# One-hots of a decoder layer's expert selection: each token's values contiguous, indices and gates held twice

## The chip, the cores and the metric

The kernel runs on one core of one Trainium2 chip. Time is device time of one execution in microseconds. Before the change the median of three runs is 1737.91 us (1737.27 to 1738.87). One execution was recorded by the hardware profiler; all rows and traces below come from such recordings.

## The reference

One decoder layer for 256 tokens of width 2048: an input projection, two groups of attention heads, an output projection with residual and LayerNorm, then retrieval over 128 x 128 = 16384 experts of one neuron each, and a second LayerNorm. What matters here is the retrieval:

```python
qh = (xc @ wq).reshape(TOKEN_CHUNK, PEER_HEADS, 2, PEER_HALF)
s1 = jnp.einsum('chd,nd->chn', qh[:, :, 0], sk1)      # 128 scores, s2 likewise
v1, i1 = lax.top_k(s1, PEER_TOPK)                     # 16 best of each half
cand = v1[..., :, None] + v2[..., None, :]
cidx = i1[..., :, None] * PEER_NKEYS + i2[..., None, :]
top_s, pos = lax.top_k(cand, PEER_TOPK)               # 16 of the 256 sums
eidx = jnp.take_along_axis(cidx, pos, axis=-1)
g = jax.nn.softmax(top_s, axis=-1)
h = jnp.einsum('cd,chkd->chk', xc, u[eidx])
a = jax.nn.gelu(h) * g
y = jnp.einsum('chk,chkd->cd', a, v[eidx])
```

So each token selects 8 heads x 16 = 128 experts, each with a gate g. An expert's number is i1 * 128 + i2.

## The kernel before

All names and lines are those of the program printed at the end of this section. Operations are recorded through a helper (line 116), so profile rows carry line 116 and are told apart by the names of tiles; a trailing number is cut from a name there (`oh1` and `oh2` are `oh`, `iota16` is `iota`).

**Dense stream.** The work is a list of units, each one block of 1 MB of weights. A unit is loaded by SyncE's DMA queue (`raw`), split into a high and a low part (`wh` by a ScalarE cast, `wl` by a VectorE subtraction of 128 x 1024, two per unit) and multiplied on TensorE in four steps of 8 f32 matmuls (`psb<-xx,wh` and `psb<-xx,wl`). A load is issued three units ahead, a split is made two units ahead. At a unit's end ScalarE and VectorE fold its result (`ev`, `bl`). The first 32 units of the retrieval (`use_u`) take all tokens against 32 x 128 experts; the units after them (`use_c`) take gathered rows of the remaining experts, which only a list names; their weights are turned by four TensorE transposes per step.

**Jobs between the steps.** Small work is written as generators. After each step of a unit the recorder calls `pump` (line 235), which lets a job go one piece on, if a planner's clocks (`Paced`, lines 71 to 118) say that ScalarE and VectorE are no more than a slack behind TensorE, and if the job's own due time has passed. The clocks advance by a cost formula for each operation (`cost`, line 78). So the costs that the formula gives set the order in which instructions stand; the chip runs each engine's instructions in that order.

**Where the planner's order is overridden.** When a unit needs indices that the list has not given yet, `column` (line 179) calls `pump` without a slack until it has them. There the jobs are written one after the other with no dense work between; this text calls such a place a hold.

**The gates** (`job_gate`, line 878). For every token and every one of its 128 slots the kernel has i1, i2 and g. Transposed, slots lie on the 128 partitions: `iT` [128, 2, 256] holds i1 and i2 in f16, one value per token; `gpc` [128, 2, 256] holds the gate times 2^15 as an f16 value and an f16 remainder.

**One-hots** (`one_hots`, line 933). For a group of four tokens VectorE makes `oh2`, where i2 equals 0..127, and `oh1`, where i1 does; where gates are wanted also `og`, which is `oh1` times each of the two parts of the gate. `oh2` is [128, 4, 128]: a token's 128 values are neighbours. `oh1` is [128, 128, 4]: the four tokens are innermost, so a token's 128 values lie 4 elements apart; its comparison is against a table `iotab` that holds each number four times. `og` is [128, 2, 128, 4] in the same way.

**Products.** Per token, TensorE multiplies `oh2` (as weights) by `oh1` and adds over tokens: how often each expert is selected (`job_count`, line 978; 4 matmuls per group). By `og`, main part and remainder, it makes the token's 128 x 128 table of gates (`gate_mm`, 8 matmuls per group), which ScalarE copies to `stg`. All are of 128 columns. After 32 groups `stg` goes to memory in 16 stores of 512 KB (`gtab`, `job_store`, line 968) on SyncE's queue, which also issues the units' loads. `job_count` walks all 64 groups, with gates for the first 32 only; its products run two groups behind its one-hots, `oh1` and `oh2` have three buffers, `og` two. `job_gates` (line 1001) makes the other 32 groups of gates later, between list rounds.

**The list** (`job_list`, line 1020). From the counts VectorE sorts the experts, and then, in rounds, names 3 x 128 of them at a time: comparisons `sg`, f16 matmuls `psa<-dx,sg` of 130 neighbouring columns, a copy `i2l` on ScalarE, and four VectorE instructions (`at`, `lw`). One copy `i2l` marks one round.

Of the kernel before, what the change touches and what calls it, by code (L numbers as in the profile page):

```python
# [13 lines left out]
F16 = mybir.dt.float16  # L14
# [3 lines left out]
OP = mybir.AluOpType  # L18
AX = mybir.AxisListType

P = 128
S = 256
# [99 lines left out]
def layer_kernel(ctx: ExitStack, tc: tile.TileContext, xT, x, win, wo, wq, ut, un, v, lams, sublng,  # L122
# [4 lines left out]
    PE, ACT, DVE, POOL = (Paced(e, n, clk, done_at) for e, n in ((nc.tensor, "PE"), (nc.scalar, "ACT"),  # L127
                                                       (nc.vector, "DVE"), (nc.gpsimd, "POOL")))
# [11 lines left out]
    def psA():  # L140
        return pa.tile([P, 512], F32, name="psa", tag="a")

    def psB():
        return pb.tile([P, 512], F32, name="psb", tag="b")
# [733 lines left out]
    def job_gate():  # L878
        while keep.get("nhead", 0) < NH:
            yield  # L880
        s = tv2.rearrange("p t h k -> p (t h) k")
        w = tk.tile([P, 2 * NH, 16], F32, name="w")
        DVE.tensor_tensor(w, s, s[:, :, 0:1].to_broadcast([P, 2 * NH, 16]), op=OP.subtract)
        ACT.activation(w, w, AF.Exp)
        DVE.tensor_copy(ei, eid.rearrange("p t h k -> p t (h k)"))
        eh = tk.tile([P, 2, 2, P], I32, name="eh")
        DVE.tensor_scalar(eh[:, 0], ei, 7, None, op0=OP.logical_shift_right)
        DVE.tensor_scalar(eh[:, 1], ei, P - 1, None, op0=OP.bitwise_and)
        DVE.tensor_copy(i12, eh)
        yield  # L890
        DVE.tensor_reduce(gs, w, axis=AX.X, op=OP.add)
        DVE.reciprocal(gs, gs)
        DVE.tensor_tensor(w, w, gs[:, :, None].to_broadcast([P, 2 * NH, 16]), op=OP.mult)
        yield
        for t in range(2):
            ps = psA()
            for i in range(2):
                PE.transpose(ps[:, i * P:(i + 1) * P], i12[:, i, t], ident)
            PE.transpose(ps[:, 2 * P:3 * P], w.rearrange("p (t h) k -> p t (h k)", t=2)[:, t], ident)
            c = slice(t * P, (t + 1) * P)  # L900
            ACT.copy(iT[:, :, c], ps[:, :2 * P].rearrange("p (i s) -> p i s", i=2))
            ACT.copy(gT[:, c], ps[:, 2 * P:3 * P])
            yield
        DVE.tensor_scalar(gT, gT, GSCALE, None, op0=OP.mult)
        DVE.tensor_copy(gpc[:, 0], gT)
        DVE.tensor_tensor(gpc[:, 1], gT, gpc[:, 0], op=OP.subtract)
        keep["gate"] = True
        yield

# [22 lines left out]

    def one_hots(q, gated):

        k = slice(4 * q, 4 * q + 4)
        oh2 = main.tile([P, 4, P], F16, name="oh2", tag="oh2", bufs=3)
        oh1 = main.tile([P, P, 4], F16, name="oh1", tag="oh1", bufs=3)
        DVE.tensor_tensor(oh2, iota16[:, None].to_broadcast([P, 4, P]), iT[:, 1, k, None].to_broadcast([P, 4, P]),
                          op=OP.is_equal)
        DVE.tensor_tensor(oh1, iotab, iT[:, 0, None, k].to_broadcast([P, P, 4]), op=OP.is_equal)  # L940
        og = None
        if gated:
            og = main.tile([P, 2, P, 4], F16, name="og", tag="og", bufs=2)
            DVE.tensor_tensor(og, oh1[:, None].to_broadcast([P, 2, P, 4]),
                              gpc[:, :, None, k].to_broadcast([P, 2, P, 4]), op=OP.mult)
        return oh2, oh1, og

    def gate_mm(oh2, og):
        ps = psA()
        for c in range(4):  # L950
            for p in range(2):
                PE.matmul(ps[:, c * P:(c + 1) * P], oh2[:, c], og[:, p, :, c], start=(p == 0), stop=(p == 1))
        return ps

    def gate_out(gp, q, ps):

        t, k = divmod(4 * q, P)
        if k == 0:
            stgs[t] = gp.tile([P, NEXP, P], F32, name="stg", tag="stg", bufs=1)
        stg = stgs[t]  # L960
        ACT.activation(stg[:, :, k:k + 4].rearrange("p j c -> p c j"), ps.rearrange("p (c j) -> p c j", c=4), AF.Copy,
                       scale=1.0 / GSCALE)
        if k == P - 4:
            start(job_store(t, stg))
# [13 lines left out]
    def job_count(gp):  # L978


        cnt, ohs, ps, n = psA(), {}, {}, S // 4
        for q in range(n + 2):
            if q < n:
                ohs[q] = one_hots(q, q < n // 2)
            r = q - 2
            if r >= 0:
                oh2, oh1, og = ohs.pop(r)
                for c in range(4):
                    t, k = divmod(4 * r + c, P)
                    PE.matmul(cnt[:, t * P:(t + 1) * P], oh2[:, c], oh1[:, :, c], start=(k == 0), stop=(k == P - 1))  # L990
                if og is not None:
                    ps[r] = gate_mm(oh2, og)
            if r - 1 in ps:
                gate_out(gp, r - 1, ps.pop(r - 1))
            yield -1.0e9
        c2 = cnt[:, :2 * P].rearrange("p (t j) -> p t j", t=2)
        DVE.tensor_scalar(some, c2, 0.5, None, op0=OP.is_gt)
        DVE.tensor_scalar(once, c2, 1.0, None, op0=OP.is_equal)
        keep["count"] = True
# [477 lines left out]
    for n, (part, b) in enumerate(order):  # L1477
        one = part[0] == "S"
        add_unit(None, use_v(n, one, halves[n]), kind="S" if one else "V", part=part, b=b, halves=halves[n],
                 s=int(part[1]) * NS + b if one else 0)  # L1480
# [18 lines left out]

    main = ctx.enter_context(tc.tile_pool(name="main", bufs=1))  # L1500
    iota16 = main.tile([P, P], F16, name="iota16")
    iotab = main.tile([P, P, 4], F16, name="iotab")
    iT = main.tile([P, 2, S], F16, name="iT")
    gpc = main.tile([P, 2, S], F16, name="gpc")
    some = main.tile([P, 2, P], F16, name="some")
    once = main.tile([P, 2, P], F16, name="once")
    row = main.tile([P, P], F32, name="row")
# [21 lines left out]
    gT = tk.tile([P, S], F32, name="gT")  # L1529

    POOL.iota(iota50, pattern=[[1, NCAND]], base=0, channel_multiplier=0, allow_small_or_imprecise_dtypes=True)
    POOL.iota(iota16, pattern=[[1, P]], base=0, channel_multiplier=0, allow_small_or_imprecise_dtypes=True)
    POOL.iota(iotab, pattern=[[1, P], [0, 4]], base=0, channel_multiplier=0, allow_small_or_imprecise_dtypes=True)
    SP.dma_start(gtab[PADROW:, 0:P], zero.bitcast(F32))
    SP.dma_start(gtab[PADROW:, P:S], zero.bitcast(F32))
    run_units(n_wq, SLACK_TOPK)
# [5 lines left out]
    with tc.tile_pool(name="gp", bufs=1, side="right") as gp:  # L1542
        st["gates"] = pos["k"] + 2
        start(job_list(ls))
        start(job_count(gp))
        start(job_gates(gp))
        while "gates" not in keep:
            run_units(pos["k"] + 1, SLACK_GATE)
# [24 lines left out]
    with tc.If(again > 0):  # L1573
        xf = [strm.tile([P, D], F32R, name=f"w{i}", tag=f"w{i}") for i in "hl"]
        for t in range(2):
            xr = strm.tile([P, D], F32, name="raw", tag="raw")
            SP.dma_start(xr, x1d[t * P:(t + 1) * P])
            for q in range(4):
                ps = psA()
                for i in range(4):  # L1580
                    k = 4 * q + i
                    PE.transpose(ps[:, i * P:(i + 1) * P], xr[:, k * P:(k + 1) * P], ident)
                ACT.copy(xf[t].bitcast(F32)[:, q * 512:(q + 1) * 512], ps)
        for j in range(NEXP):
# [4 lines left out]
            ps = psB()  # L1589
            for t in range(2):  # L1590
                for k in range(NK):
                    c = slice(k * P, (k + 1) * P)
                    PE.matmul(ps[:, t * P:(t + 1) * P], wr[:, c], xf[t].bitcast(F32)[:, c],
                              start=(k == 0), stop=(k == NK - 1))
# [6 lines left out]
        for j in range(NEXP):  # L1601
# [4 lines left out]
            for t in range(2):  # L1606
                for c in range(4):
                    PE.matmul(yps[t][c], ar[:, t * P:(t + 1) * P], vr[:, c * 512:(c + 1) * 512],
                              start=(j == 0), stop=(j == NEXP - 1))
# [61 lines left out]
```

## Time and profile before

| what | value |
|---|---|
| median of 3 runs | 1737.91 us |
| profiled execution | 1734.11 us |
| its span, first to last instruction | 1732.2 us |
| TensorE clock granted, mean | 0.968 |
| busy: TensorE, VectorE, ScalarE, GpSimd | 93%, 75%, 47%, 34% of the span |
| counting, with gates | about 588 to 680 us |
| counting, without gates | about 680 to 739 us |
| sort of the list | about 739 to 777 us |
| gates of the other 32 groups | 817 to 938 us |

A row of the chain or the timeline gives start, length, engine, line, operation, tiles written and read, shapes and count; in brackets stands how long the engine was idle before it and what ended that. A row of a stage gives its ends, its length, and the busy time and count of each engine, then granted clock, DMA share and GB/s. A row of a tile gives the count and the shortest, median and longest duration in ns. Durations of neighbouring instructions overlap, so what an instruction costs its engine is read from start to start.

### The profile page before, as it was taken

How to read it: one execution, taken by the hardware profiler on the slowest of the kernel's cores; microseconds unless marked ns; L12 is line 12 of the kernel's file. 1: busy time of each engine (PE TensorE's matmuls, PEld its weight loads, DVE VectorE, ACT ScalarE, POOL GpSimd, SP SyncE). 2: the span in 40 equal slices, each digit the busy share in tenths (PEclk: the TensorE clock that was granted, in tenths of full speed). 3: DMA queues.
4: the chain of work that ended last, by engine and by line, in shares of the span. 5: the costliest groups of instructions: out<-in, count | busy, mean ns of one | idle time of the engine just before them, and what ended most of it. 6: DMA issues, size and time to landing. Idle time of an engine off the chain costs nothing.

```text
span 1732.2 us, 25235 instructions
## 1 busy us (share of the span) xinstructions
PE 1606.4 (93%) x9151; PEld 1364.4 (79%) x9151; DVE 1307.0 (75%) x2844; ACT 817.7 (47%) x1370; POOL 596.5 (34%) x558
## 2 busy tenths in 40 slices
PE   7999999998989899959979899999979999999994
PEld 6888888877878788849969788888857777788872
DVE  5686767656999887875976667786678888777767
ACT  5445555445424565323635333344445555555533
POOL 0033100015778400002001033334566666556742
PEclk9999999999989999979979899999999999999998
DMA  7454454545444434926324878798999999998861
GB/s 275 163 178 146 150 190 147 217 178 194 161 147 165 171 110 132 300 68 208 111 74 154 250 287 341 272 392 311 419 351 406 387 389 381 372 331 310 300 255 55
DMA packets 112531, 409.18 MB, mean 236 GB/s; under 512 B 11216, under 2 KB 62608, under 8 KB 69648
## 3 DMA queue, kind: packets, MB, share of 16 engines
q0 software_dynamic: 37856, 246.96, 37.4%
q1 hardware_dynamic: 74400, 160.27, 27.2%
q8 instruction: 74, 1.21, 0.3%
q14 instruction: 57, 0.47, 0.1%
q10 hardware_dynamic: 144, 0.26, 0.0%
HBM read 376.00 MB, written 31.39 MB: 235 GB/s over the span
## 4 chain that ended last, share of the span: by engine, by line
PE 64%; DVE 20%; DMA 6%; issue 4%; ACT 3%; POOL 2%; SPq 0%; DVEq 0%; ACTq 0%; POOLq 0%
PE psa L116 34%; PE psb L116 31%; DVE wl L116 6%; DVE oh L116 2%; ACT wh L116 2%; POOL gsr L187 1%; DMA gr<-gtab,aidx 1%; DMA sr<-x1d,xidx 1%; DVE lw L116 1%; DMA raw<-in_v_dram,vidx 1%; DVE tv L116 1%; DVE ti L116 1%; DVE yacc L116 1%; DVE eid L116 1%; DVE og L116 1%
## 5 line engine op out<-in xcount | busy, mean ns | idle before, releaser
L116 PE MATMUL psb<-xx,wh 128*128 128x512 f32 (+1 forms) x1407 | 504.8, 393 | 0.0
L116 DVE TENSOR_TENSOR wl<-raw,wh 128x1024 fp32r<-128x1024 f32 (+2 forms) x278 | 321.6, 1172 | 101.8 <-ACT wh L116 101.5
L116 PE MATMUL psb<-xx,wl 128*128 128x256 f32 x1392 | 373.6, 283 | 5.2 <-DVE wl L116 3.9
L116 ACT CAST wh<-raw 128x1024 fp32r<-128x1024 f32 (+1 forms) x278 | 283.5, 1044 | 65.4 <-PE psa L116 26.8
L116 PE MATMUL psa<-xx,wh 128*128 128x512 f32 x800 | 291.1, 407 | 9.4 <-DVE xx L116 8.3
L116 PEld LDWEIGHTS psb<-xx,wh 128*128 128x128 f32 x1407 | 268.3, 192 | 36.1
L116 PEld LDWEIGHTS psb<-xx,wl 128*128 128x128 f32 x1392 | 266.8, 192 | 11.3 <-DVE wl L116 5.4
L187 POOL DMA_INDIRECT raw<-in_un_dram,vidx x54 | 54.7, 1014 | 480.3 <-PE psa L116 252.1
L116 PE MATMUL psa<-xx,wl 128*128 128x256 f32 x800 | 219.2, 284 | 0.9 <-DVE wl L116 0.8
L116 DVE TENSOR_TENSOR wl<-psa,wh 128x512 fp32r<-128x512 f32 x216 | 146.6, 686 | 75.2 <-ACT wh L116 74.7
L116 ACT CAST wh<-psa 128x512 fp32r<-128x512 f32 x216 | 126.6, 587 | 149.9 <-PE psa L116 147.8
L116 PEld LDWEIGHTS psa<-xx,wh 128*128 128x128 f32 x800 | 151.0, 192 | 42.9 <-ACT wh L116 10.0
L116 PEld LDWEIGHTS psa<-xx,wl 128*128 128x128 f32 x800 | 153.9, 192 | 6.6 <-DVE wl L116 2.1
L116 DVE TENSOR_TENSOR wl<-rawv,wh 128x1024 fp32r<-128x1024 f32 x106 | 125.7, 1222 | 28.3 <-ACT wh L116 25.7
L116 PE MATMUL psa<-ident,raw 128*128 128x128 f32 x864 | 130.7, 274 | 3.4 <-DMA raw<-in_un_dram,vidx 3.4
L116 ACT CAST ah<-ar 128x256 fp32r<-128x256 f32 (+1 forms) x82 | 30.3, 370 | 201.3 <-DVE ar L116 192.3
L116 PE MATMUL psb<-wl,ah 128*128 128x512 f32 x276 | 110.2, 399 | 7.2 <-DVE wl L116 7.2
L116 PE MATMUL psb<-wh,ah 128*128 128x512 f32 x276 | 110.3, 400 | 3.4 <-DVE bl L116 2.6
L116 PEld LDWEIGHTS psa<-ident,raw 128*128 128x128 f32 x864 | 103.7, 142 | 11.8 <-issue 3.7
L116 PE MATMUL psa<-wh,ah 128*128 128x512 f32 x268 | 106.7, 398 | 4.9 <-ACT wh L116 4.9
L116 PE MATMUL psa<-wl,ah 128*128 128x512 f32 x268 | 107.7, 402 | 3.0 <-DVE wl L116 2.6
L116 PE MATMUL psb<-wh,al 128*128 128x512 f32 x276 | 109.1, 395 | 0.0
(305 smaller groups left out, 3050.7 us busy)
## 6 DMA issues: line engine op xcount, KB each, us to landing
raw<-in_win_dram SPq DMA_DIRECT2D x42, 1024.0 KB, 4.9
raw<-in_ut_dram SPq DMA_DIRECT2D x32, 1024.0 KB, 5.1
raw<-in_wo_dram SPq DMA_DIRECT2D x18, 1024.0 KB, 4.9
raw<-in_wq_dram SPq DMA_DIRECT2D x16, 1024.0 KB, 4.9
gtab<-stg SPq DMA_DIRECT2D x32, 512.0 KB, 5.4
cdr<-bl SPq DMA_DIRECT2D x39, 128.0 KB, 4.6
ar<-cdr SPq DMA_DIRECT2D x39, 128.0 KB, 7.1
hd<-bl SPq DMA_DIRECT2D x32, 128.0 KB, 1.7
```

The costliest lines, as they stand in the source:

```text
L116: return f(*a, **k)
L187: nc.gpsimd.indirect_dma_start(dst, None, src, bass.IndirectOffsetOnAxis(ap=index, axis=0))
```

## The change

`oh1` and `og` now have a token's 128 values as neighbours, as `oh2` has: [128, 4, 128] and [128, 2, 4, 128]. The products read them with a step of 1 in place of 4. `iT` and `gpc` hold each value twice, side by side ([128, 2, 256, 2]), and the comparisons read 128 values as 64 pairs: the pair of equal indices is read 64 times against pairs of 0..127. Both one-hots are made this way, against `iota16`; the table `iotab` is gone. `og` is made by two instructions of 512 elements in place of one of 1024.

```diff
-            ACT.copy(iT[:, :, c], ps[:, :2 * P].rearrange("p (i s) -> p i s", i=2))
+            ACT.copy(iT[:, :, c], ps[:, :2 * P].rearrange("p (i s) -> p i s", i=2)[..., None].to_broadcast([P, 2, P, 2]))
...
-        DVE.tensor_copy(gpc[:, 0], gT)
-        DVE.tensor_tensor(gpc[:, 1], gT, gpc[:, 0], op=OP.subtract)
+        g2 = gT[..., None].to_broadcast([P, S, 2])
+        DVE.tensor_copy(gpc[:, 0], g2)
+        DVE.tensor_tensor(gpc[:, 1], g2, gpc[:, 0], op=OP.subtract)
...
+        pairs = lambda z: z.rearrange("p c (a b) -> p c a b", b=2)
         oh2 = main.tile([P, 4, P], F16, name="oh2", tag="oh2", bufs=3)
-        oh1 = main.tile([P, P, 4], F16, name="oh1", tag="oh1", bufs=3)
-        DVE.tensor_tensor(oh2, iota16[:, None].to_broadcast([P, 4, P]), iT[:, 1, k, None].to_broadcast([P, 4, P]),
-                          op=OP.is_equal)
-        DVE.tensor_tensor(oh1, iotab, iT[:, 0, None, k].to_broadcast([P, P, 4]), op=OP.is_equal)
+        oh1 = main.tile([P, 4, P], F16, name="oh1", tag="oh1", bufs=3)
+        for i, oh in ((1, oh2), (0, oh1)):
+            DVE.tensor_tensor(pairs(oh), pairs(iota16[:, None]).to_broadcast([P, 4, P // 2, 2]),
+                              iT[:, i, k, None].to_broadcast([P, 4, P // 2, 2]), op=OP.is_equal)
         og = None
         if gated:
-            og = main.tile([P, 2, P, 4], F16, name="og", tag="og", bufs=2)
-            DVE.tensor_tensor(og, oh1[:, None].to_broadcast([P, 2, P, 4]),
-                              gpc[:, :, None, k].to_broadcast([P, 2, P, 4]), op=OP.mult)
+            og = main.tile([P, 2, 4, P], F16, name="og", tag="og", bufs=2)
+            for p in range(2):
+                DVE.tensor_tensor(pairs(og[:, p]), pairs(oh1), gpc[:, p, k, None].to_broadcast([P, 4, P // 2, 2]),
+                                  op=OP.mult)
...
-                PE.matmul(ps[:, c * P:(c + 1) * P], oh2[:, c], og[:, p, :, c], start=(p == 0), stop=(p == 1))
+                PE.matmul(ps[:, c * P:(c + 1) * P], oh2[:, c], og[:, p, c], start=(p == 0), stop=(p == 1))
...
-                    PE.matmul(cnt[:, t * P:(t + 1) * P], oh2[:, c], oh1[:, :, c], start=(k == 0), stop=(k == P - 1))
+                    PE.matmul(cnt[:, t * P:(t + 1) * P], oh2[:, c], oh1[:, c], start=(k == 0), stop=(k == P - 1))
...
-    POOL.iota(iotab, pattern=[[1, P], [0, 4]], base=0, channel_multiplier=0, allow_small_or_imprecise_dtypes=True)
```

The planner's formula gives other costs for the new instructions, so later instructions move too. Up to the gates of the second 32 groups only the forms differ. VectorE at the start of the counting, before (`oh_5511` is `oh2`, `oh_5512` is `oh1`):

```order
L116 TENSOR_SCALAR ones<-lw 128x128
L116 TENSOR_TENSOR oh_5511<-iota_3638,iT 128x512
L116 TENSOR_TENSOR oh_5512<-iotab,iT 128x512
L116 TENSOR_TENSOR og<-oh_5512,gpc 128x1024
L116 TENSOR_TENSOR wl<-raw,wh 128x1024
```

and now:

```order
L116 TENSOR_SCALAR ones<-lw 128x128
L116 TENSOR_TENSOR oh_5509<-iota_3638,iT 128x512
L116 TENSOR_TENSOR oh_5510<-iota_3638,iT 128x512
L116 TENSOR_TENSOR og<-oh_5510,gpc 128x512 x2
L116 TENSOR_TENSOR wl<-raw,wh 128x1024
```

The places are the same; `og` is two instructions. The first hold, where dense units wait for the list, is seen on ScalarE, whose `stg` copies mark groups of gates and whose `i2l` copies mark list rounds. Before:

```order
L116 COPY ev<-psb 128x256
L116 CAST wh<-psa 128x512
L116 ACTIVATE stg<-psa 128x4x128
L116 COPY i2l<-psa 128x3
L116 ACTIVATE stg<-psa 128x4x128 x3
L116 COPY i2l<-psa 128x3
L116 ACTIVATE stg<-psa 128x4x128 x3
L116 COPY i2l<-psa 128x3
L116 ACTIVATE stg<-psa 128x4x128 x3
L116 COPY i2l<-psa 128x3
L116 ACTIVATE stg<-psa 128x4x128
```

and now:

```order
L116 COPY ev<-psb 128x256
L116 CAST wh<-psa 128x512
L116 ACTIVATE stg<-psa 128x4x128 x3
L116 COPY i2l<-psa 128x3
L116 ACTIVATE stg<-psa 128x4x128 x3
L116 COPY i2l<-psa 128x3
L116 ACTIVATE stg<-psa 128x4x128 x3
L116 COPY i2l<-psa 128x3
L116 ACTIVATE stg<-psa 128x4x128 x3
L116 COPY i2l<-psa 128x3
L116 ACTIVATE stg<-psa 128x4x128
```

Two groups and one list round that stood among dense work stand in the hold now: on TensorE 14 groups are left before it (15 before the change), 12 stand in it (10), 6 behind it (7). The second hold, some 36 steps of dense work later, before:

```order
L116 COPY ev<-psb 128x256
L116 CAST wh<-psa 128x512
L116 COPY i2l<-psa 128x3 x5
L116 CAST wh<-psa 128x512
L116 ACTIVATE bl<-bl 128x256
```

and now:

```order
L116 COPY ev<-psb 128x256
L116 CAST wh<-psa 128x512
L116 COPY i2l<-psa 128x3 x6
L116 CAST wh<-psa 128x512
L116 ACTIVATE bl<-bl 128x256
```

It has one round more.

More of the change, by code (lines that the diff above doesn't have):

```diff
@@ L1501, in layer_kernel @@
     iota16 = main.tile([P, P], F16, name="iota16")
-    iotab = main.tile([P, P, 4], F16, name="iotab")
-    iT = main.tile([P, 2, S], F16, name="iT")
-    gpc = main.tile([P, 2, S], F16, name="gpc")
+    iT = main.tile([P, 2, S, 2], F16, name="iT")
+    gpc = main.tile([P, 2, S, 2], F16, name="gpc")
     some = main.tile([P, 2, P], F16, name="some")
```

## The prediction

> **What bounds the kernel now.** I read the page first, then the chain of waits inside the stages that the diff touches, then the order of work on VectorE there. TensorE carries the kernel:
>
> ```profile
> PE 1606.4 (93%) x9151; PEld 1364.4 (79%) x9151; DVE 1307.0 (75%) x2844; ACT 817.7 (47%) x1370; POOL 596.5 (34%) x558
> PE 64%; DVE 20%; DMA 6%; issue 4%; ACT 3%; POOL 2%; SPq 0%; DVEq 0%; ACTq 0%; POOLq 0%
> ```
>
> The diff touches 588 to 739 us (the counting, whose first 32 groups also build gates) and 817 to 938 us (the other 32 groups of gates). The chain in the counting, first with gates, then without (start, length, what):
>
> ```profile
> 591.65 1.40 PE psa L116 x12
> 593.05 1.40 PE psb L116 x8
> 594.45 1.39 PE psa L116 x12
> ...
> 688.35 0.46 PE psa L116 x4
> 688.81 1.39 PE psb L116 x8
> 690.20 0.46 PE psa L116 x4
> ```
>
> It is TensorE without a gap: 12 (later 4) f16 matmuls on one-hots, then 8 matmuls of the dense stream, over and over. One f16 matmul with its weights takes 1.395/12 = 0.116 us. So any gain in the counting has to come from TensorE, and VectorE must be able to follow. VectorE over one unit of four groups:
>
> ```profile
> 620.05 0.42 DVE L116 TENSOR_TENSOR bl<-psb,ev 128x256 f32<-128x256 f32 x1 [1.09 <-ACT ev L116]
> 620.39 0.68 DVE L116 TENSOR_TENSOR oh<-iota,iT 128x512 f16<-128x512 f16 x1
> 620.99 0.42 DVE L116 TENSOR_TENSOR oh<-iotab,iT 128x512 f16<-128x512 f16 x1
> 621.51 0.69 DVE L116 TENSOR_TENSOR og<-oh,gpc 128x1024 f16<-128x1024 f16 x1
> 622.12 1.22 DVE L116 TENSOR_TENSOR wl<-raw,wh 128x1024 fp32r<-128x1024 f32 x1
> 623.25 0.68 DVE L116 TENSOR_TENSOR oh<-iota,iT 128x512 f16<-128x512 f16 x1
> ...
> 631.21 0.42 DVE L116 TENSOR_TENSOR bl<-psb,ev 128x256 f32<-128x256 f32 x1 [1.09 <-ACT ev L116]
> ```
>
> From start to start a group costs 0.60 + 0.52 + 0.61 = 1.73 us (an instruction's last 0.08 us overlaps the next one's start; `og` waits 0.10 for its input), a `wl` 1.13, a `bl` 0.34. A unit has 0.34 + 4 x 1.73 + 2 x 1.13 = 9.5 us of it, in a period of 11.16: 1.6 us spare. By stage (columns: PE, PEld, DVE, ACT, POOL busy, clock, DMA share, GB/s):
>
> ```profile
> 590.00:680.00 90.00, 90.00 (x646) 80.58 (x645) 76.05 (x125) 53.55 (x66) 0.00 (x0) 1.00 0.33 116
> 686.40:730.90 44.50, 44.50 (x290) 37.74 (x290) 38.65 (x68) 15.47 (x25) 0.00 (x0) 1.00 0.96 298
> 817.00:868.40 51.40, 49.84 (x400) 47.07 (x399) 46.89 (x110) 29.83 (x51) 5.09 (x5) 1.00 0.33 115
> 868.40:890.80 22.40, 11.90 (x90) 9.61 (x90) 20.24 (x63) 8.56 (x12) 0.00 (x0) 0.58 0.00 1
> 917.00:938.00 21.00, 20.94 (x153) 19.14 (x152) 17.36 (x42) 12.28 (x20) 1.87 (x2) 1.00 0.36 128
> 958.00:981.00 23.00, 15.35 (x94) 12.40 (x93) 15.66 (x79) 4.90 (x14) 0.00 (x0) 0.79 0.91 263
> ```
>
> Without gates the DMA is full (0.96); from 817 TensorE and VectorE are both near full; from 868 TensorE stands while VectorE finishes list rounds and gates (the first hold), again from 966 for list rounds alone (the second).
>
> **What one matmul will cost.** No row has these matmuls with neighbouring columns, but the list's f16 matmuls (130 columns, neighbouring, weights loaded the same way) stand right beside the gates':
>
> ```profile
> 844.24 0.33 PE L116 MATMUL psa<-dx,sg 128*128 128x130 f16 x3
> 844.42 1.08 PE L116 MATMUL psa<-og,oh 128*128 128x128 f16 x8
> ...
> 956.63 0.33 PE L116 MATMUL psa<-dx,sg 128*128 128x130 f16 x3
> ...
> 957.09 0.28 PE L116 MATMUL psb<-xx,wl 128*128 128x256 f32 x1
> 957.21 0.39 PE L116 MATMUL psb<-xx,wh 128*128 128x512 f32 x1
> 957.44 0.28 PE L116 MATMUL psb<-xx,wl 128*128 128x256 f32 x1
> ```
>
> Three start within 0.18 us: at most 0.06 each, I take 0.058, half of 0.116. The one difference that I see is that before, a token's 128 values lie 4 apart. So 0.058 us goes per matmul. Part comes back at the switch to the f32 stream: from the three at 956.63 to the `wl` at 957.09 are 0.46 us, against 3 x 0.058 + 0.23 (957.21 to 957.44) = 0.40; with the slow matmuls that extra is about 0.02, so I charge 0.04 per switch. The bounds are 0 and 0.058 saved, and the neighbour speaks for the upper one.
> [...]
>
> **What one one-hot will cost.**
>
> ```profile
> L116 DVE TENSOR_TENSOR oh<-iota,iT x96: 678/682/687, 587.7 to 933.5; 128x512 f16<-128x512 f16 x96
> L116 DVE TENSOR_TENSOR oh<-iotab,iT x96: 411/417/475, 588.3 to 934.1; 128x512 f16<-128x512 f16 x96
> L116 DVE TENSOR_TENSOR og<-oh,gpc x64: 691/692/748, 588.7 to 934.6; 128x1024 f16<-128x1024 f16 x64
> ...
> L116 DVE TENSOR_TENSOR oh<-iota,pf x16: 974/980/2357, 441.8 to 563.2; 128x800 f32<-128x800 f32 x16
> ```
>
> The same 512 elements take 682 ns where the index is one value repeated, and 417 where it comes in rows of four neighbours; 1024 take 692. So rows of neighbours run twice as fast (265 ns for 512, plus about 150 fixed). The change reads rows of two, equal, neighbours, 64 times: no row has that. The bounds are 417 and 682. I take 417: rows of four read again 128 times have it, and repeating one word each step is not what slows (`oh<-iota,pf` repeats one f32 word at 800 elements in 980 ns, one a cycle like the 682 row).
> [...]
>
> A group is then 0.34 + (0.34 + 0.10, the wait of `og`, + 0.08) + 0.34 + 0.34 = 1.54 us in place of 1.73 (four instructions of 417 less 0.08), and without gates 0.68 in place of 0.94.
>
> **The sum, stage by stage.**
> 1. Preparation. The copies of indices and gates write twice the elements:
>
> ```profile
> L116 DVE CAST gpc<-gT x1: 293/293/293, 582.9 to 582.9; 128x256 f16<-128x256 f32 x1
> L116 DVE TENSOR_TENSOR gpc<-gT,gpc x1: 425/425/425, 583.2 to 583.2; 128x256 f16<-128x256 f32 x1
> ```
>
> Between nothing and double, 0.7 us, plus ScalarE's two `iT` copies. TensorE has dense work until 591.6, which hides most; uncovered, it is late one-hots. I charge 0.6. The dropped index table was GpSimd's, long before: 0.
> 2. Counting with gates, 8 units. TensorE per unit: 11.16 - 4 x (12 x 0.058 - 0.04) = 8.5. VectorE: 0.34 + 4 x 1.54 + 2.27 = 8.8. So VectorE takes over. A ring of two `og` and a lookahead of two groups pass delays on; I take 9.0 (bounds 8.8 and 9.5, today's VectorE sum): 8 x 2.16 = **17.3** (13 to 19).
> 3. Counting without gates, 8 units. TensorE: period 7.41, less 4 x (4 x 0.058 - 0.04) = 6.6. VectorE 5.3. The DMA needs 0.96 x 7.41 = 7.1, so a backlog of 0.5 us a unit builds behind the stores of the gate table:
>
> ```profile
> raw<-in_ut_dram SPq DMA_DIRECT2D x9, 1024.0 KB, 7.3
> ...
> 688.33 0.94 SPq L177 DMA_DIRECT2D raw<-in_ut_dram  x1
> ...
> 699.82 1.05 ACT L116 CAST wh<-raw 128x1024 fp32r<-128x1024 f32 x1
> ```
>
> A load lands 7.3 us after its issue and is first used 11.5 after it: the slack of 4 covers 8 x 0.5. I take **6.0** of 8 x 0.8 = 6.4 (2.4 if the DMA sets the pace). The sort that follows moves as it stands.
> 4. 817 to 868. One gate group and one list round move out into the hold. TensorE's work falls by 14 x (8 x 0.058 - 0.04) + 0.93 + 0.17 = 7.1 of 51.4; VectorE's 46.9 by 14 x 0.19 + 1.73 + 1.8 = 6.2. TensorE still sets it at 44.3; I take **6.5** (3 to 7).
> 5. The first hold. VectorE gets two groups and one round more:
>
> ```profile
> 880.79 0.95 PE L116 MATMUL psa<-dx,sg 128*128 128x130 f16 x6 [2.37 <-DVE sg L116]
> 887.94 0.95 PE L116 MATMUL psa<-dx,sg 128*128 128x130 f16 x6 [2.37 <-DVE sg L116]
> 976.70 0.95 PE L116 MATMUL psa<-dx,sg 128*128 128x130 f16 x6 [1.85 <-DVE sg L116]
> ```
>
> From 880.79 to 887.94 are 7.15 us for three groups and one round: 3 x 1.73 leaves 2.0 for the round. So 2 x 1.54 + 2.0 - 10 x 0.19 = 3.2 us longer: **-3.2**. Nothing hides it, the dense units behind wait for the list.
> 6. 891 to 938: six groups in place of seven, TensorE full: 0.93 + 6 x 0.42 = **3.5**.
> 7. The second hold has six rounds in place of five: 0.95 + 1.85 = 2.8, less 0.2 for the round that no longer stands in the stream: **-2.6**.
>
> Sum: 17.3 + 6.0 + 6.5 - 3.2 + 3.5 - 2.6 - 0.6 = 26.9 us. The profiled execution took 1734.1 us (span 1732.2), so it would give 1707.2; the median of the runs, 1737.9, is 3.8 above it, and gives **1711.0**.
>
> **Rivals.**
> - The repeated pair runs at the single rate (682 ns, 0.60 from start to start). A group is 2.50 us. Stage 2: 0.34 + 10.0 + 2.27 = 12.6 a unit, 8 x 1.45 = 11.6 lost; stage 3: VectorE 7.4, nothing gained; stage 4: 46.9 + 14 x 0.77 - 3.5 = 54.2 against 51.4, 2.8 lost; first hold 2 x 2.50 + 2.0 + 10 x 0.77 = 14.7 lost; then +0.8, -2.6, -0.6. Together 31.5 lost: **1769**, slower. It decides from about 0.58 us an instruction on. For it: no 16-bit row of two in the trace. Against: the 417 row.
> - Halfway, 549 ns: a group 1.98, a unit 10.5: 5.0 + 6.0 + 4.5 - 8.5 + 3.5 - 2.6 - 0.6 = 7.3 gained, **1731**. [...]
> - The stride costs TensorE nothing, and the 0.116 has another cause: stages 2 and 3 gain nothing, stage 4 1.1, stage 6 0.9, the holds and the preparation take 6.4: **1742**, same or slightly slower. Against it stand two kinds of matmul side by side at 844. [...]
>
> **How the numbers follow.** Forecast 0.84, single rate 0.06, halfway 0.05, free stride 0.05. This kernel's runs tell 0.2% (3.5 us) from no change. Faster 0.84 + 0.05 (1731) = 0.89; slower 0.06 + 0.02; same 0.03. With the bounds of the stages, good together: 19 + 6.4 + 7 - 3 + 4 - 2.6 = 31 gained, 1707; bad together: 13 + 2.4 + 3 - 5 + 2.5 - 3 - 0.6 = 12, 1726. Since the low end may gain a little more where both engines are near full, the range is 1703 to 1726.
>
> **What would show it.** The one-hots of both kinds at 417 ns and `og` twice 417; the twelve f16 matmuls in 0.7 us where 1.40 stood; the period of a unit 9.0 and 6.6; waits of TensorE for `og` in stage 2, which has none now; no wait of `wh` for loads in stage 3; a first hold of about 25.6 us, a second of one round more. One-hots over 0.58 us, or matmuls still 0.11 apart, make the forecast wrong.

## The result and the profile after

The change takes the kernel from 1738.39 to 1710.73 us (medians of four runs each): ratio 0.9837, 95% interval 0.9818 to 0.9856, a gain of 27.7 us. The profiled execution of the changed kernel is the slowest of its four (1714.49 us, span 1712.4), that of the kernel before is faster than all of its timed ones (1734.11). The pair of traces therefore shows only 19.6 us, and the difference of 8 us needs an explanation of its own (below).

The head of the page, busy times and the chain by engine:

```profile
PE 1580.7 (92%) x9151; PEld 1334.9 (78%) x9151; DVE 1285.7 (75%) x2908; ACT 815.8 (48%) x1370; POOL 599.5 (35%) x557
PE 67%; DVE 19%; DMA 5%; issue 3%; ACT 3%; POOL 1%; SPq 0%; DVEq 0%; ACTq 0%; POOLq 0%
```

TensorE still carries it and is busy 26 us less; the 64 more VectorE instructions are the second gate products. The chain of waits in the counting, with gates at its beginning and in its middle, then without gates (start, length, what):

```profile
592.29 0.69 PE psa L116 x12
592.97 1.45 PE psb L116 x8
594.42 0.69 PE psa L116 x12
...
617.47 1.14 DVE wl L116
618.61 0.68 DVE oh L116 x2
...
619.38 0.76 DVE og L116 x2
620.14 0.68 DVE oh L116 x2
...
661.44 0.24 PE psa L116 x4
661.68 1.45 PE psb L116 x8
663.13 0.24 PE psa L116 x4
```

Twelve f16 matmuls take 0.69 us where 1.40 stood, and four take 0.24 where 0.46 stood. The eight dense matmuls behind them take 1.45 where 1.39 to 1.40 stood: that is what the switch to f32 gives back, 0.055 us. From 608 to 637 the chain runs through VectorE; the rows of its tiles show what an instruction costs there (count, shortest/median/longest ns, first and last start):

```profile
L116 DVE TENSOR_TENSOR oh<-iota,iT x192: 411/417/422, 588.3 to 906.8; 128x512 f16<-128x512 f16 x192
L116 DVE TENSOR_TENSOR og<-oh,gpc x128: 415/424/427, 589.1 to 907.7; 128x512 f16<-128x512 f16 x128
L116 DVE CAST gpc<-gT x1: 426/426/426, 582.6 to 582.6; 128x512 f16<-128x512 f32 x1
L116 DVE TENSOR_TENSOR gpc<-gT,gpc x1: 693/693/693, 583.1 to 583.1; 128x512 f16<-128x512 f32 x1
```

Rows of two equal values, read 64 times over, run like the rows of four neighbours of before: 417 ns for 512 in both one-hots, and 424 in the gate products. The two copies of the gates cost 426 and 693 ns instead of 293 and 425. By stage (columns: length, busy time and instructions of PE, PEld, DVE, ACT, POOL, then clock, DMA share, GB/s):

```profile
592.30:661.40 69.10, 68.93 (x642) 59.32 (x640) 65.98 (x149) 50.52 (x64) 0.00 (x0) 1.00 0.41 140
661.40:713.70 52.30, 52.30 (x375) 43.45 (x373) 41.58 (x87) 21.17 (x33) 0.00 (x0) 1.00 1.01 316
791.00:835.40 44.40, 42.99 (x387) 40.04 (x387) 40.20 (x116) 28.32 (x50) 4.86 (x5) 1.00 0.40 143
835.40:862.80 27.40, 15.18 (x126) 12.15 (x126) 24.68 (x89) 10.96 (x17) 0.00 (x0) 0.59 0.00 1
```

With gates TensorE stands for 0.2 us of 69 by its busy time and VectorE for 3: the two are nearly balanced. Without gates the DMA engines are full (share 1.01), and TensorE still never stands (busy for 52.30 of 52.30 us). The first hold is longer than before: from the last dense matmul ahead of it to the first one behind it 26.7 us, where it was 24.7; the second takes 16.4, where it was 12.7.

The gain by stage is read by laying the two traces side by side at the same matmul of the dense stream, of which both have 6831, and taking the difference of their starts:

| part, in the prediction's order | predicted us | measured us |
|---|---|---|
| 1 preparation | -0.6 | -0.6 |
| 2 counting with gates | +17.3 | +20.1 |
| 3 counting without gates | +6.0 | +5.3 |
| sort, moved as it stands | 0 | +0.1 |
| 4 up to the first hold | +6.5 | +6.2 |
| 5 first hold | -3.2 | -2.4 |
| 6 between the holds | +3.5 | +3.5 |
| 7 second hold | -2.6 | -3.9 |
| sum behind the second hold | 26.9 | 28.3 |
| from there to the end | 0 | -8.7 |
| end | 26.9 | 19.6 |

A hold's line here takes in the few dense matmuls just behind it. Up to the second hold no part is off by more than 2.8 us, and the sum by 1.4; the last line but one was not forecast.

### The profile page after: what moved, and what is told of

Its sections match the earlier page's. It is cut to its first block, busy times and chain, and to the rows that moved or that the text cites. A ratio compares the mean times of both kernels' runs of the same rounds, so it can differ in the third digit from the quotient of the medians.

```text
span 1712.4 us, 25292 instructions
## 1 busy us (share of the span) xinstructions
PE 1580.7 (92%) x9151; PEld 1334.9 (78%) x9151; DVE 1285.7 (75%) x2908; ACT 815.8 (48%) x1370; POOL 599.5 (35%) x557
## 4 chain that ended last, share of the span: by engine, by line
PE 67%; DVE 19%; DMA 5%; issue 3%; ACT 3%; POOL 1%; SPq 0%; DVEq 0%; ACTq 0%; POOLq 0%
PE psa L116 34%; PE psb L116 34%; DVE wl L116 6%; DVE oh L116 2%; ACT wh L116 2%; DVE og L116 1%; DVE lw L116 1%; DMA raw<-in_v_dram,vidx 1%; DVE ti L116 1%; DVE yacc L116 1%; DMA raw<-in_win_dram 1%; DMA raw<-in_un_dram,vidx 1%; DVE tv L116 1%; DVE eid L116 1%; DVE cand L116 1%
## 5 line engine op out<-in xcount | busy, mean ns | idle before, releaser
L116 PE MATMUL psb<-xx,wh 128*128 128x512 f32 (+1 forms) x1407 | 510.6, 397 | 0.3 <-issue 0.3
L187 POOL DMA_INDIRECT raw<-in_un_dram,vidx x54 | 59.6, 1103 | 457.8 <-PE psa L116 242.6
L116 DVE TENSOR_TENSOR wl<-psa,wh 128x512 fp32r<-128x512 f32 x216 | 146.7, 687 | 89.3 <-ACT wh L116 78.5
```

The source lines that it names most:

```text
L116: return f(*a, **k)
L187: nc.gpsimd.indirect_dma_start(dst, None, src, bass.IndirectOffsetOnAxis(ap=index, axis=0))
```

## The experiments

Three questions: are the stages' gains due to the causes that the prediction named; what do the holds owe to the order; and is the loss behind the second hold the change's own? The kernel before was run beside each batch, with medians of 1741.52 us (first four kernels) and 1742.65 us (last four).

### The change once more

No edit. The kernel of the change, for a second trace and closer times.

> The changed kernel once more, nothing edited. In its first profile 28 us were won by the end of the second hold and only 19.6 were left at the end, while the medians are 27.7 us apart. Theory A (the 9 us lost between 1000 and 1300 us are variation of single runs, stretches at half the TensorE clock and late gathers among them): the median stays near 1711 us, and this profile loses less than 5 us behind the second hold against the profile of before. Theory B (whoever comes earlier to the gathered rows waits for the DMA there): this profile loses 8 us or more there again, at the same units.

Measured: 1714.46 us, ratio 0.9841 [0.9819, 0.9864], so the gain is confirmed. In its trace the gain behind the second hold is 28.9 us, and by 1250 us of the kernel before it has fallen to 19.5: 9.4 us are lost again, the size that the second theory expected. But its cause is not there. TensorE's waits for gathered rows between 980 and 1310 us (total, times, longest), in the first profile of the kernel before and in this one:

```profile
PE psa L116 <- DMA raw<-in_un_dram,vidx: 3.4, 2, 2.3
```

```profile
PE psa L116 <- DMA raw<-in_un_dram,vidx: 3.6, 3, 2.3
```

And the time is lost elsewhere than in the first trace of the change: that one loses it in small steps, this one 6.2 us at one place, where TensorE stutters (1.7 us in three gaps for which the profile names no releaser), waits 2.5 us for a list round and then runs at half speed. In the first profile of the kernel before this wait is 1.3 us, and the rest is missing. The chain there:

```profile
1095.95 0.24 DVE sg L116
1096.19 0.05 issue
1096.24 1.41 PE psa L116 x9
1097.65 2.67 PE psb L116 x8
1100.32 0.85 PE psa L116 x4
1101.17 2.11 PE psb L116 x8
1103.28 0.44 PE psa L116 x4
```

Eight dense matmuls take 2.67 us instead of 1.4. The granted clock of this stretch is the last but two of the columns:

```profile
1095.80:1102.60 6.80, 6.36 (x26) 5.51 (x27) 5.94 (x12) 1.00 (x2) 2.75 (x4) 0.50 0.79 273
```

In 6.8 us at a clock of 0.50 about 3.4 us of work are lost (an estimate, 6.8 x 0.5), more than in the wait. The first theory had asked for a loss of less than 5 us, and this trace does not give it; what speaks for it comes from the next run. The median is 3.5 us above the 1711 that it named, beside a kernel before that is 3.1 us slower than then.

### The kernel before once more

No edit. A second profile of the kernel before, to see whether the loss after 980 us needs the change at all.

> The kernel before once more, for a second profile of it. Theory A (the 5 to 9 us that all profiles of changed kernels lose between 980 and 1250 us come from waits that fall differently each time and from stretches of half clock behind them; the first profile of before had none): this profile has a granted clock of 0.98 to 0.99 in that stretch and takes 270 to 277 us for it, and its span is 1736 us or more. Theory B (the loss belongs to the change): the stretch takes 267 us at clock 1.00 again.

Measured: one execution, 1743.57 us, span 1741.7. The same 1120 dense matmuls (the 3840th to the 4960th), in the first profile of before, in this one, and in the second one of the change:

```profile
981.80:1248.90 267.10, 255.34 (x1796) 230.93 (x1795) 191.11 (x444) 109.55 (x246) 96.64 (x100) 1.00 0.86 328
```

```profile
985.00:1258.60 273.60, 260.99 (x1796) 233.94 (x1795) 191.47 (x444) 108.57 (x246) 98.31 (x100) 0.99 0.84 320
```

```profile
952.90:1229.40 276.50, 261.66 (x1796) 234.88 (x1795) 191.73 (x446) 108.90 (x246) 100.73 (x99) 0.98 0.84 319
```

The unchanged kernel loses 6.5 us in this stretch against its own first profile, with a clock of 0.99, as the theory of variation had it. (The other 3 us of its longer span are lost before the counting, 2 of them in the first 30 us.) 5.7 of the 6.5 us are lost at one place, the same as above. In the first profile of the kernel before and in that of the change any two changes of the clock lie a whole multiple of 3.41 us apart, and a stretch at half clock lasts from 3.41 to 23.89 us. Here are four steps of 3.4 us of this execution (columns as before, the clock the last but two):

```profile
1117.70:1121.10 3.40, 2.11 (x8) 1.12 (x7) 0.00 (x0) 0.20 (x1) 0.94 (x1) 1.00 0.80 287
1121.10:1124.50 3.40, 3.40 (x13) 2.92 (x13) 2.92 (x4) 2.43 (x6) 0.00 (x0) 0.50 0.85 286
1124.50:1127.90 3.40, 1.84 (x16) 1.29 (x15) 3.33 (x9) 0.58 (x1) 1.47 (x2) 1.00 0.42 109
1127.90:1131.30 3.40, 3.40 (x14) 3.00 (x13) 3.40 (x4) 0.63 (x2) 0.41 (x1) 0.50 0.81 287
```

and the step with the same work in the first profile of the kernel before, with its wait for the list round:

```profile
1117.93:1121.35 3.42, 2.22 (x17) 1.79 (x18) 3.39 (x10) 0.95 (x2) 1.87 (x2) 1.00 0.91 323
```

```profile
1120.16 1.44 PE psb L116 x8
```

In the second profile TensorE stutters ahead of the list round (1.3 us in four gaps for which the profile names no releaser), then waits 1.6 us for the round, and after each of the two a step at half clock follows, which by its clock of 0.50 costs about 1.7 us (an estimate, 3.4 x 0.5). In the first profile the stutter is missing, the wait is 1.3 us, the step around it is busy for 2.22 us, and the clock stays at 1.00. Steps that were busy for 2.11 and 1.84 us were followed by half clock here.
Busy time alone does not decide it. In the first profile of the kernel before, the steps from 1025.77 and 1039.42 us were busy for 1.84 and 1.85 us, and the clock stayed at 1.00. Over that profile and the one of the change, of the steps at full clock that were busy for at most 1.56 us all 24 were followed by half clock, of those from 1.61 to 2.01 us four of nine, and of those busy for longer none of 896; the step of 2.11 us above, in another execution, was. What decides from 1.61 us on is not shown.

All other traces of this study take 270 to 277 us for these matmuls, those of the kernels with the old matmul times (below) among them with 273 and 276: the first profile of the kernel before is the odd one. So most of the loss is not the change's. The remaining 2.9 us lie within what two traces of one kernel differ by here; whether a part of them belongs to the change stays open.

### The order of before

The planner is told the old costs, so that it puts the gate groups and the list rounds where they were (10 groups and 3 rounds in the first hold, 5 rounds in the second), and the cheap one-hots stay.

```
@@ estimate of an instruction @@
-    n = max(_free(a) for a in aps)
+    n = max(_free(a) for a in aps) * self.clk.get("scale", 1.0)
...
-            return (n + 66) / 0.96
+            return (n + 66 * self.clk.get("fixed", 1.0)) / 0.96
@@ one_hots @@
+                clk["fixed"] = 1.0 - p
                 DVE.tensor_tensor(pairs(og[:, p]), ...)
+            clk["fixed"] = 1.0
...
```

In the lines left out `scale` is 0.5 for the copies of indices and gates, which now write twice the elements.

> The changed kernel, but the planner charges the new instructions what it charged the old ones, so that everything stands in the order of before: three list rounds and ten groups in the first hold, five rounds in the second. If the holds cost what the prediction says (3.2 us less what stands before it, and 2.6 us), this is 4 to 8 us faster than the change: 1703 to 1707 us. Rival (VectorE carries that stretch either way, so a round costs the same inside and outside of a hold): the same as the change, 1710 to 1712 us.

Measured: 1709.51 us, ratio 0.9816 [0.979, 0.9842]: 5 us below the change beside it (1714.46), though the intervals overlap. The gain on the kernel before, which is slower here than when the expectation was made (1741.52, not 1737.9), is 32 us, and the expected times made it 31 to 35. The traces bear out the difference to the change: from 800 us of the kernel before to the end of the second hold this order gains 8.6 us on it (+3.9 up to the first hold, +1.5 in it, +2.3 behind it, +0.9 at the second), the planner's new order, in the trace of the run above, 3.5 (+6.1, -2.3, +3.3, -3.6). Just ahead, behind the sort, this order loses 0.6 us. TensorE's stretches without dense matmuls take 23.3 and 12.7 us, against 26.7 and 16.1. What the new order gains ahead of a hold it pays in it, and more.

### The first one-hot in pairs, alone

The kernel before, with only the contiguous one-hot `oh2` reading its index in pairs; the other one and the gate products stay four apart.

```
-            ACT.copy(iT[:, :, c], ps[:, :2 * P].rearrange("p (i s) -> p i s", i=2))
+            ACT.copy(iT[:, 0, c], ps[:, :P])
+            ACT.copy(iT2[:, c], ps[:, P:2 * P, None].to_broadcast([P, P, 2]))
...
-        DVE.tensor_tensor(oh2, iota16[:, None].to_broadcast([P, 4, P]), iT[:, 1, k, None].to_broadcast([P, 4, P]),
-                          op=OP.is_equal)
+        DVE.tensor_tensor(pairs(oh2), pairs(iota16[:, None]).to_broadcast([P, 4, P // 2, 2]),
+                          iT2[:, k, None].to_broadcast([P, 4, P // 2, 2]), op=OP.is_equal)
```

> The kernel before, with only the comparison for oh2 made in pairs (i2 held twice); oh1, og, their layout and the products stay as before, and so does the order. If TensorE's stride is what was paid for: the counting keeps its periods (11.16 and 7.41 us a unit), f16 matmuls 0.116 us apart, and only the hold wins 10 x 0.26 us: 1734 to 1737 us. Rival (the gain comes from VectorE's faster one-hots): 1715 to 1725 us.

Measured: 1736.95 us, ratio 0.9971 [0.9955, 0.9988]. The one-hot takes 418 ns as expected, and the counting with gates does not move:

```profile
592.25:681.50 89.25, 89.25 (x642) 79.95 (x640) 66.62 (x122) 53.07 (x66) 0.00 (x0) 1.00 0.31 110
```

VectorE is down to 66.6 of 89.3 us, TensorE full as before. A cheaper one-hot alone is worth nothing in the counting. The medians make its gain 4.6 us, where 1 to 4 were expected of a kernel before at 1737.9. In its trace it gains 3.7 us between 817 and 981 us of the kernel before, 2.7 of it in the first hold: ten one-hots that cost VectorE 0.26 us less each, in an unchanged order, so VectorE sets that hold. (As a whole the trace is 3.6 us longer than the first one of the kernel before, because it too loses 6 us between 1000 and 1250.)

### One-hots contiguous, indices and gates held once

From the change: the layout for TensorE stays, the pairs go, and the planner is told the old costs, so that the order is that of before.

```
-        for i, oh in ((1, oh2), (0, oh1)):
-            DVE.tensor_tensor(pairs(oh), pairs(iota16[:, None]).to_broadcast([P, 4, P // 2, 2]),
-                              iT[:, i, k, None].to_broadcast([P, 4, P // 2, 2]), op=OP.is_equal)
+        DVE.tensor_tensor(oh2, iota16[:, None].to_broadcast([P, 4, P]), iT[:, 1, k, None].to_broadcast([P, 4, P]),
+                          op=OP.is_equal)
+        DVE.tensor_tensor(oh1, iota16[:, None].to_broadcast([P, 4, P]), iT[:, 0, k, None].to_broadcast([P, 4, P]),
+                          op=OP.is_equal)
...
-    iT = main.tile([P, 2, S, 2], F16, name="iT")
-    gpc = main.tile([P, 2, S, 2], F16, name="gpc")
+    iT = main.tile([P, 2, S], F16, name="iT")
+    gpc = main.tile([P, 2, S], F16, name="gpc")
```

> The kernel before, with oh1 and og laid out as the change has them (a token's 128 values are neighbours) but made from indices and gates that are held once; order as before. Theory: the matmuls are 0.058 us apart, and yet VectorE's instructions for oh1 and og take 682 ns each, a group 2.50 us, a unit with gates 12.6 us in place of 11.2; with the holds some 28 us slower than before: 1760 to 1772 us. Rival (neighbours for TensorE are the whole gain, VectorE has room): 1710 to 1720 us.

Measured: 1780.26 us, ratio 1.0224 [1.0197, 1.0252], slower than before, by more than expected (39 us; the range made it 22 to 34). The rows of its tiles:

```profile
L116 DVE TENSOR_TENSOR oh<-iota,iT x192: 672/684/739, 587.6 to 972.7; 128x512 f16<-128x512 f16 x192
L116 DVE TENSOR_TENSOR og<-oh,gpc x128: 683/689/694, 588.9 to 974.1; 128x512 f16<-128x512 f16 x128
```

This is what the rival of the single rate would have been. With the matmuls at 0.06 us and the one-hots at 684 ns a unit with gates takes 13.0 us, all VectorE's, against 11.16 before, and one without gates 7.4, as before. So 14 us go in the counting, where 12.6 us a unit would have made it 11.5; up to the first hold another 10 go, 11 in it, and 4.5 behind it. The expectation gave these three no shares, so where the rest of it fell short is open.

### Runs of two, and every second value

Two layouts between the old one (a token's values 4 apart) and the new one (neighbours), both with the order of before and all one-hots in pairs. In the first, TensorE reads two neighbours and skips six values; in the second, it reads every second value.

```
@@ runs of two @@
-        oh1 = main.tile([P, 4, P], F16, name="oh1", tag="oh1", bufs=3)
+        oh1 = main.tile([P, P // 2, 4, 2], F16, name="oh1", tag="oh1", bufs=3)
...
-                PE.matmul(ps[:, c * P:(c + 1) * P], oh2[:, c], og[:, p, c], start=(p == 0), stop=(p == 1))
+                PE.matmul(ps[:, c * P:(c + 1) * P], oh2[:, c], og[:, p, :, c], start=(p == 0), stop=(p == 1))
@@ every second value @@
+        oh1 = main.tile([P, 2, P, 2], F16, name="oh1", tag="oh1", bufs=3)
...
+                PE.matmul(ps[:, c * P:(c + 1) * P], oh2[:, c], og[:, p, c // 2, :, c % 2], start=(p == 0), stop=(p == 1))
```

> The change with the gate groups in the places they had before, and each token's 128 values of oh1 and og laid in 64 runs of two, the four tokens' runs side by side: TensorE reads 4 bytes, skips 12, reads 4. Nothing is left out. Theory (only the strided read slows a matmul, and a run of two is still strided): a matmul takes 0.116 us as before, the unit with gates stays at 11.16 us and the unit without at 7.41, and only VectorE's gain is left, as when the first one-hot alone is made fast: 1733 to 1738 us, ratio about 0.997. Rival 1 (runs of one 4-byte word are enough): a matmul takes 0.058, the units 8.7 and 6.75, the time of the order of before, 1706 to 1713 us. Rival 2 (half the loss): 0.087 a matmul, 1720 to 1725 us. The one-hots should take about 420 ns in all three.

> The change with the gate groups in the places they had before, and oh1 and og laid out with two tokens side by side: TensorE reads every second 2-byte value. Nothing is left out. Theory A (what counts is how many values of one row lie in 16 bytes: 8 neighbours full rate, 2 half rate, so 4 might still be full): a matmul takes 0.058 us, units 8.7 and 6.75, 1706 to 1713 us. Theory B (any stride halves the rate): 0.116 us, units 11.16 and 7.41, 1733 to 1738 us. The one-hots should take about 420 ns in both.

Measured: runs of two 1738.82 us, ratio 0.9978 [0.9967, 0.9989]; every second value 1709.91 us, ratio 0.9809 [0.9788, 0.983]. The chain with gates, first for runs of two:

```profile
603.44 1.40 PE psb L116 x8
604.84 1.40 PE psa L116 x12
606.23 1.39 PE psb L116 x8
607.63 1.39 PE psa L116 x12
```

and for every second value:

```profile
601.86 0.71 PE psa L116 x12
602.57 1.45 PE psb L116 x8
604.01 0.71 PE psa L116 x12
604.72 1.44 PE psb L116 x8
```

The one-hots take 417 ns in both. Runs of two keep TensorE at 0.116 us a matmul and leave the units at 11.16 and 7.41; the time is 0.8 us above the expected range, beside a kernel before that is slower as well, and the ratio is the expected one. Every second value gives 0.059 and units of 8.65 and 6.76, like neighbours. So it is not the stride as such, and not whether values come in pairs. With four values of a row in 16 bytes, as in the second, a matmul took 0.059 us, about as with neighbours (0.0575); with two in 16 bytes, in runs (the first) or apart (the kernel before), it took 0.116. Three were not tried, nor four in two runs of two; the count in 16 bytes fits all four layouts, and no run shows it to be the cause.

### Both one-hots in one instruction

From the change: the two one-hots of a group are one VectorE instruction of 1024 values, the two gate products another; the planner orders them by its own costs.

```
-        for i, oh in ((1, oh2), (0, oh1)):
-            DVE.tensor_tensor(pairs(oh), pairs(iota16[:, None]).to_broadcast([P, 4, P // 2, 2]),
-                              iT[:, i, k, None].to_broadcast([P, 4, P // 2, 2]), op=OP.is_equal)
+        DVE.tensor_tensor(pairs(oh), pairs(iota16[:, None]).to_broadcast([P, 8, P // 2, 2]),
+                          iT[:, q].rearrange("p i c b -> p (i c) b")[:, :, None].to_broadcast([P, 8, P // 2, 2]),
+                          op=OP.is_equal)
+        oh1, oh2 = oh[:, 0:4], oh[:, 4:8]
...
-            for p in range(2):
-                DVE.tensor_tensor(pairs(og[:, p]), pairs(oh1), gpc[:, p, k, None].to_broadcast([P, 4, P // 2, 2]),
-                                  op=OP.mult)
+            DVE.tensor_tensor(pairs2(og), pairs2(oh1[:, :, None].to_broadcast([P, 4, 2, P])),
+                              gpc[:, k, :, None].to_broadcast([P, 4, 2, P // 2, 2]), op=OP.mult)
```

> From the change: both one-hots of a group in one VectorE instruction of 1024 values, and both gate products in another, in place of four of 512; the order is the one that the planner then writes (9 groups in place of 12 in the first hold, 4 list rounds in place of 6 in the second). Nothing is left out. A group costs VectorE about 0.61 + 0.10 + 0.61 = 1.32 us in place of 1.54. If the unit with gates (8.64 us) is set by VectorE (8.75 by the chain in its second half) it falls to TensorE's 4 x (0.69 + 1.45) = 8.56; the holds are shorter by 3 x 1.54 + 9 x 0.22 = 6.6 us and by two rounds of 1.9, of which about 2 us come back as matmuls that now lie ahead of or behind a hold: 1714.5 - 0.7 - 6.6 - 3.8 + 2 = 1705 us, range 1702 to 1709. Rival (the holds are set by the list rounds' chain through TensorE and ScalarE, not by VectorE's one-hots): 1710 to 1715 us, no better than the change.

Measured: 1706.15 us, ratio 0.9793 [0.9768, 0.9817]. It beats the kernel before and, by intervals that do not touch, the change (0.9819 to 0.9864); its median is the lowest of all, with the order of before and every second value within its interval's reach. Its one-hots, and its counting with gates:

```profile
L116 DVE TENSOR_TENSOR oh<-iota,iT x96: 674/683/689, 588.7 to 893.6; 128x1024 f16<-128x1024 f16 x96
```

```profile
592.15:660.47 68.32, 68.32 (x642) 59.17 (x641) 63.55 (x90) 50.83 (x66) 0.00 (x0) 1.00 0.43 146
```

1024 values take 683 ns, 150 less than two instructions of 417. From start to start the gain is smaller. One group on VectorE:

```profile
617.18 0.68 DVE L116 TENSOR_TENSOR oh<-iota,iT 128x1024 f16<-128x1024 f16 x1
617.97 0.69 DVE L116 TENSOR_TENSOR og<-oh,gpc 128x1024 f16<-128x1024 f16 x1
618.58 0.68 DVE L116 TENSOR_TENSOR oh<-iota,iT 128x1024 f16<-128x1024 f16 x1
```

That is 1.40 us, where the change takes 1.53 (618.53 to 620.06) and 1.32 were expected: two instructions already overlap, and `og` waits for its input. The unit with gates falls from 8.64 to 8.54 us, and TensorE no longer stands at all: that is its own sum, 4 x (0.69 + 1.45) = 8.56. So 0.1 us a unit was what VectorE still cost in the change. The rest comes from the holds: against the kernel before the first hold gains 5.4 us where the change lost 2.4, and the second gains 1.9 where it lost 3.9. Some of that goes into the stretches around them, 4.9 gained ahead of the first hold where the change gained 6.2, and 1.3 between the two where it gained 3.5. Most of this is the order: three groups fewer stand in the first hold than in the change and two rounds fewer in the second, and nine groups that are 0.13 us cheaper make only 1.2 us. So this run does not refute the rival's reason by itself. For the first hold the kernel with one fast one-hot does, in an unchanged order. The second has no one-hots, and there the rival has a point: in the change a round takes 2.81 us, of which VectorE waits 0.82 for TensorE and 0.23 for ScalarE.

## Why the prediction was right

- **The matmul (0.058 us) and its reason.** Measured 0.69/12 = 0.0575 with gates and 0.24/4 = 0.06 without. The neighbour row with 130 columns was the right witness. The reason given, values 4 apart, holds for the kernel before; every second value (0.059 us) shows that it is not any distance that counts.
- **The switch to f32 (0.04 us).** Measured 0.055, from 1.395 to 1.45. This and the 0.06 make the unit without gates 4 x (0.24 + 1.45) = 6.76 (measured 6.75) instead of 6.6, and the term 3 came to 5.3 instead of 6.0. The DMA did not set the pace, though its share is 1.01: the slack of 4 us held, since TensorE never stood there.
- **The one-hot (417 ns).** Measured 417 and 424 for rows of two equal values. Between the rows of 512 and of 800 values that the choice leaned on (682 and 980 ns) lie 1.03 ns a value; no trace shows a cycle. The kernel that holds indices and gates once shows what hung on it: 71 us against the other kernel in the order of before (1780.26 and 1709.51).
- **Counting with gates (9.0 us a unit).** The mis-sized term: 8.64 measured, 2.8 us over the stage. The two sums were right (TensorE 8.5 predicted, 8.56 by the chain; VectorE 8.8, and 8.75 from one `wl` on the chain at 608.73 to the one at 617.47). The 0.2 charged for delays passed on between two nearly equal engines did not come. Instead TensorE ran at its own pace for the first sixteen groups (2.13 us each from start to start), on one-hots made ahead, and the units behind them took VectorE's 8.75: TensorE loses 0.2 us a unit (8.75 against 8.56), and its weight loads wait for `og` (13 times between 600 and 664 us, 2.0 us in all). The chain goes through VectorE from 608 to 637. That VectorE "takes over" was therefore half right; the kernel with two instructions a group, where these waits are gone, shows the whole price of VectorE over the stage, 0.1 us a unit.
- **Up to the first hold, and between the holds.** 6.2 for 6.5 and 3.5 for 3.5.
- **The holds.** -2.4 for -3.2 and -3.9 for -2.6, together -6.3 for -5.8. In the second, the chain shows what the term left out:

```profile
935.25 0.19 DVE ki L116
...
936.78 0.17 DVE aidx L116
936.96 0.24 DVE sg L116
937.24 0.96 PE psa L116 x6
```

Ten short VectorE instructions that make the indices of the gathers (`ki` to `aidx`, 1.6 us) stand between a round's end and the next comparison `sg`, and TensorE waits 3.4 us there, not 1.85. In the kernel before they ran from 961.7 to 963.4, among dense work ahead of the hold. The new order moved them in with the round, and the prediction counted the round alone. That the holds are dearer because the planner moved groups and rounds into them was tested by the order of before, which turns -2.4 and -3.9 into +1.5 and +0.9.

- **The late loss.** Not in the prediction, which let everything behind the second hold move as it stands. In the pair of traces it is 8.7 us, and 6.5 are in the kernel before as well when it is profiled again. The forecast stood all the same because it was made against the median: the 3.8 us between before's profiled execution and its median, taken over unexplained, are likely of this kind (no trace of the median runs exists). From the sum and the profiled execution alone it would have been 1707.2 us, and the profiled execution of the change took 1714.49.
- **How close it came.** 26.9 us forecast and 27.7 measured is in part luck: counting with gates gained 2.8 us more than charged, and counting without gates, the way to the first hold and the second hold fell short by 2.3 together.
- **Rivals.** The single rate and the halfway rate fall by the 417 ns, the free stride by 0.0575 and by the runs of two.

## What to carry to other kernels

Where two kinds of matmul of nearly the same shape stand side by side in a trace with different times, compare first how their operands lie; here that was the difference, and the faster row (at most 0.06 us a matmul, beside 0.116) was the price after the change of layout (0.0575). When an operation becomes cheap, look at what the planner does with it: here it moved work into the holds and gave back about 5 us that the old order keeps (in the traces, and in medians whose intervals overlap). And set one profiled execution against the spread of the runs before reading a difference of a few us between two traces as the change's.

## What the runs showed of the hardware that was not expected

- TensorE streams f16 nearly as fast when it reads every second value (0.059 us for 128 columns) as when it reads neighbours (0.0575), and at half that rate when it reads two neighbours out of every eight (0.116), as it does with one out of four.
- VectorE takes a repeated pair of 16-bit values at the rate of neighbouring ones (417 ns for 512 and 692 for 1024 in the kernel before), though one 4-byte word is read 64 times running: 417 ns for 512 values, 683 for 1024, so by the difference 266 ns for 512 more and, as an estimate, about 150 fixed.
- The granted clock fell to 0.50 for 3.4 us after steps of 3.4 us in which TensorE was busy for 2.11 or 1.84 us (the kernel before, second profile). By that clock each such step costs about 1.7 us. Steps about as busy kept the full clock in the first profile of the same kernel (1.84, 1.85 and 2.22 us). The two executions differ by 5.7 us at that place, and busy time alone does not tell which of them loses.
